# Five input projections of a diffusion block by seven block products instead of eight, with their results kept in DRAM

## The chip, the cores and the metric

One Trainium2 chip, one core of it. The metric is the device time of one execution in microseconds. Three runs of the kernel before took 1818.68, 1819.56 and 1820.62 us (median 1819.56).

## The reference, cut to what matters

One block of a diffusion model on 1024 latent tokens and 256 context tokens, width 1024, all in fp32. `h` is the normed and modulated input, 1024 x 1024.

```python
u, v, q, k, vv, r, af, ab, ga, gb = split(h @ w_in)
b_lat = rmsnorm(gla_scan(q, k, vv, gates(af, ab))) * gla_norm_g * silu(r)     # 4 heads, both directions
v     = layernorm(gelu(v))
a_lat = gelu(u) * (einsum('gpq,bnqgc->bnpgc', w_spatial, v) + b_spatial)
y     = sigmoid(ga) * (a_lat @ w_branch_a) + sigmoid(gb) * (b_lat @ w_branch_b)
x     = x + g1 * (y @ w_out)
a, g  = split(modulate(rmsnorm(x)) @ w_ffn_in)
x     = x + g2 * ((silu(g) * a) @ w_ffn_out)
out   = rmsnorm(x)
```

u, v, r, ga and gb are five products of 1024 x 1024 x 1024 each. g1, g2 and the shifts and scales come from `silu(c) @ w_ada`.

## The kernel before, in words

Every fp32 product is made of three passes of a faster format: each operand is split into a high part (a rounding copy on ACT) and a low part (a subtraction on DVE), and high x high, high x low and low x high are summed in PSUM (`PASS`, L261). A weight tile of 1024 rows by 128 columns is loaded, split by `split_w` (L223 to L231) and multiplied by `mm_fm` (L263 to L266) against the feature-major activations `hT`: 24 matmuls of 512 columns for each half of the tokens. `fm_unit` (L285) is one such tile, 48 matmuls. `tm_unit` (L268) gives token-major results with 256 columns to a matmul; it makes the heads' values and v.

SBUF holds three kinds of buffers that matter here: 40 slots of 4 KB a partition (`slot`, L85) for operands and everything large, 3 raw weight buffers (`raw_w`), and 4 buffers for the split weights. PSUM has 8 banks in two groups of 4.

The order of the work, by program: the first modulation vectors (w_ada) and the context; the norm of x; four heads (L645 to L655, their projections one head ahead); then `gate_b` (L453), which makes r in 8 `fm_unit`s and multiplies the heads' output with silu(r); then a loop (L702) of 8 pairs of units, one for gb and one for branch b, beside which DVE makes the rest of the modulation vectors (`ada_cols`, L670: 32 loads of 512 KB, each with one multiply-add of 1024 columns); then v (L759) by `tm_unit`, beside which `weight_sums` (L742) combines blocks of w_ffn_out and stores them in DRAM, 11 steps of four loads' worth of data; then u with the spatial mixing (L784 to L818, 8 units); then ga and branch a (L841 to L854); then w_out (`project`, L870).

The feed-forward products (L906 to L1198) already use seven block products for eight: both operands are cut in 2 x 2 blocks, sums of blocks are formed and split beforehand, and seven products replace eight. For w_ffn_in, 22 "quads" of 7 x 12 = 84 matmuls each run in one hand-ordered chain on TensorE (`pe`, L863), the first four with part of their products made early while the activations' sums are formed on DVE (L1013 to L1033). w_ffn_out is done in seven `quarter`s (L1103) with operands that are loaded, combined and split on the way.

The compiler's list scheduler orders each engine's instructions by program order and by when it expects operands and buffers to be there; so work from further down may fill gaps, as far as buffers are free. DMAs are issued from SP in one queue; a store that waits for its data holds up what is behind it.

Of the kernel before, what the change touches and what calls it, by code (L numbers as in the profile page):

```python
# [17 lines left out]
P = 128  # L18
T = 1024
# [14 lines left out]
def block_kernel(  # L34
# [39 lines left out]
    small = scope.enter_context(tc.tile_pool(name="small", bufs=2))  # L74
    dram = ctx.enter_context(tc.tile_pool(name="dram", bufs=1, space=bass.MemoryType.DRAM))
# [375 lines left out]
    braw = []  # L451

    def gate_b(h):  # L453

        for fo in (2 * h, 2 * h + 1):
            def evac(ps, hf, fo=fo):
                sl = slice(hf * 512, (hf + 1) * 512)
                sr = small.tile([P, 512], F32, tag="raw", name=nm("sr"), bufs=4)
                nc.scalar.activation(sr, ps, AF.Silu)
                nc.vector.tensor_mul(braw[fo][:, sl], braw[fo][:, sl], sr)  # L460

            fm_unit(w_in, C_R + fo * P, hT.get, evac)
# [30 lines left out]
    def head(h, qq, kk, dec, v, between):  # L493
# [126 lines left out]
        braw.extend(rb)  # L620
# [23 lines left out]
    v = head_products(0, *ahead[:2])  # L644
    for h in range(HEADS):  # L645
        now, ahead = ahead, None

        def between():
            global_next.append(head_gates(h + 1) if h + 1 < HEADS else None)
# [12 lines left out]
    bs = []  # L662
    for h in range(HEADS):
        gate_b(h)
        bs += [split_act(braw[2 * h]), split_act(braw[2 * h + 1])]
# [4 lines left out]
    def ada_cols(chunk, dst):  # L670
# [9 lines left out]
        for hf in range(2):  # L680
            pb = gbank((P, 4, P))
            nc.tensor.matmul(pb, ones, acc[:, hf * 512:(hf + 1) * 512], start=True, stop=True)
            t = small.tile([P, 4, P], F32, tag="raw", name=nm("adat"), bufs=4)
# [14 lines left out]

    mods = [cst.tile([P, 8], F32, name=f"mod{i}") for i in range(4)]
    ada = (step for i in range(4) for step in ada_cols(2 + i, mods[i]))  # L700
    y = []
    for fo in range(KT):  # L702
        sg = slot([P, T])
        fm_unit(w_in, C_GB + fo * P, hT.get, lambda ps, hf: nc.scalar.activation(sg[:, hf * 512:(hf + 1) * 512], ps, AF.Sigmoid))
        [next(ada, None) for _ in range(3 if fo else 0)]

        def evac(ps, hf):
            sl = slice(hf * 512, (hf + 1) * 512)
            nc.vector.tensor_mul(sg[:, sl], ps, sg[:, sl])

        fm_unit(w_branch_b, fo * P, act_get(bs), evac)
        [next(ada, None) for _ in range(2)]
        y.append(sg)
    next(ada, None)
    g1, sh2, s2, g2 = mods
    nc.vector.tensor_scalar(s2, s2, 1.0, None, op0=ALU.add)
    nc.vector.tensor_mul(s2, s2, n2c)


    wsp = slot([P, 8, P])  # L720
    nc.sync.dma_start(wsp, w_spatial.rearrange("g p q -> p g q"))
    wspT = slot([P, 8, P])
    for hf in range(2):
        pt = gbank((P, 4, P))
        for j in range(4):
            nc.tensor.transpose(pt[:, j, :], wsp[:, 4 * hf + j, :], ident)
        nc.scalar.copy(wspT[:, 4 * hf:4 * hf + 4, :], pt)
    bsp = slot([P, 8, P])
    nc.gpsimd.dma_start(bsp.rearrange("p g q -> p (g q)"), b_spatial[0].rearrange("g q -> (g q)").partition_broadcast(P))
    for hf in range(2):  # L730
        pb = gbank((P, 4, P))
        nc.tensor.matmul(pb, ones, wspT[:, 4 * hf:4 * hf + 4, :], start=True, stop=True)
        for j in range(4):
            g = 4 * hf + j
            nc.vector.scalar_tensor_tensor(bsp[:, g, :], pb[:, j, :], lnbc[:, g:g + 1], bsp[:, g, :], op0=ALU.mult, op1=ALU.add)
# [21 lines left out]
    vg = [[slot([P, 4, 256]) for _ in range(2)] for _ in range(4)]  # L757
    stats = small.tile([P, NT, 4, 6], F32, tag="bst", name="bst", bufs=1)
    for gp in range(4):  # L759
        def evac(ps, tp):  # L760
            t = vg[gp][tp // 2][:, 2 * (tp % 2):2 * (tp % 2) + 2, :]
            nc.scalar.activation(t, ps, AF.Gelu)
            for j in range(2):
                nc.vector.bn_stats(stats[:, 2 * tp + j, gp, :], t[:, j, :])

        [next(wsums, None) for _ in range(3)]
        tm_unit(w_in, C_V + gp * 256, hT.get, NT, evac)
# [3 lines left out]
    r = rstd_of(mv[:, :, 1], NT, 1.0)  # L771
    shift = small.tile([P, NT], F32, tag="shift", name="shift", bufs=1)
    nc.vector.scalar_tensor_tensor(shift, mv[:, :, 0], -1.0, r, op0=ALU.mult, op1=ALU.mult)
    for gp in range(4):
        for tt in range(NT):
            t = vg[gp][tt // 4][:, tt % 4, :]
            if tt % 2:
                nc.scalar.activation(t, t, AF.Identity, bias=shift[:, tt:tt + 1], scale=r[:, tt:tt + 1])
            else:
                nc.vector.tensor_scalar(t, t, mv[:, tt, 0:1], r[:, tt:tt + 1], op0=ALU.subtract, op1=ALU.mult)  # L780

    as_ = [None] * KT
    late = {}
    for g in range(8):  # L784
        halves = []

        def evac(ps, hf):
            u = small.tile([P, 512], F32, tag="raw", name=nm("u"), bufs=4)
            nc.scalar.activation(u, ps, AF.Gelu)
            halves.append(u)  # L790

        fm_unit(w_in, C_U + g * P, hT.get, evac)
        if g < 4:
            as_[g] = slot([P, T], F32R), slot([P, T], F32R)
        elif g < 7:
            late[g] = slot([P, T])
        for hf in range(2):
            pm = gbank((P, 4, P))
            for j in range(4):
                nc.tensor.matmul(  # L800
                    pm[:, j, :], vg[g // 2][hf][:, j, (g % 2) * P:(g % 2) * P + P], wspT[:, g, :], start=j == 0, stop=True, skip_group_check=True
                )
            mx = small.tile([P, 4, P], F32, tag="raw", name=nm("mx"), bufs=4)
            nc.vector.scalar_tensor_tensor(mx, pm, lngc[:, g:g + 1], bsp[:, g, :].unsqueeze(1).to_broadcast([P, 4, P]), op0=ALU.mult, op1=ALU.add)
            mx = mx.rearrange("p s i -> p (s i)")
            sl = slice(hf * 512, (hf + 1) * 512)
            a = late[g][:, sl] if g in late else mx
            nc.vector.tensor_mul(a, halves[hf], mx)
            halves[hf] = a
        if g == 7:  # L810
            for i, u in late.items():
                as_[i] = split_act(u)
            as_[g] = slot([P, T], F32R), slot([P, T], F32R)
        if g not in late:
            for hf, a in enumerate(halves):
                hi, lo = (t[:, hf * 512:(hf + 1) * 512] for t in as_[g])
                nc.scalar.copy(hi, a)
# [413 lines left out]
```

## Time and profile before

| | |
|---|---|
| median of 3 runs | 1819.56 us |
| the profiled execution | 1818.25 us, its span 1816.5 us |
| TensorE (PE) busy | 1763.1 us, 97% |
| VectorE (DVE) busy | 982.9 us, 54% |
| ScalarE (ACT) busy | 599.3 us, 33% |
| GpSimd (POOL) busy | 137.5 us, 8% |
| bytes moved by DMA | 201.84 MB, mean 111 GB/s |

The span is the time from the first to the last instruction on the core. The busy shares are of the whole span; stages differ, so rows by stretch of time are needed beside them. A matmul's own duration in the profile is its way through the array (389 ns for 512 columns); matmuls overlap, so the pace is the length of a stretch over the number of matmuls in it.

### The profile page before, as it was taken

Reading aid. Unit: us, or ns where it says so; the run is one execution under the profiler, and the core shown is the slowest. Engines: PE = TensorE matmul, PEld = TensorE weight load, DVE = VectorE, ACT = ScalarE, POOL = GpSimd, SP = SyncE. Lnnn points to the kernel's source line nnn. Section 1 sums busy time; section 2 is a strip of 40 time slices with the busy share of each in tenths; the row PEclk is TensorE's granted clock in tenths of the full one; section 3 lists DMA queues with packets and bytes.
Section 4 is the critical chain, followed back from the end, with each engine's and each line's share of the span. In section 5 each row is a group of like instructions: output and inputs, shape, how many; then the busy total and the mean of one; then the engine's idle time right before and its main releaser. Section 6 shows DMA issues by size and latency. Waiting matters only on the chain. (4 is left out here: it accounts for less than half of the span.)

```text
span 1816.5 us, 22024 instructions
## 1 busy us (share of the span) xinstructions
PE 1763.1 (97%) x8786; PEld 1472.8 (81%) x8786; DVE 982.9 (54%) x1398; ACT 599.3 (33%) x892; POOL 137.5 (8%) x141
## 2 busy tenths in 40 slices
PE   8899999999999999999999999989999999899996
PEld 3887888888888889988888888768888888788885
DVE  7687463643345526553322354895545554556795
ACT  6653432423221112141211222543333332345252
POOL 2220000000000000000000000012121211100001
PEclk9999999999999999999999999999999999999998
DMA  9511001011145439811111242233222222458472
GB/s 341 147 31 35 25 23 36 24 35 35 47 139 183 145 113 320 282 42 40 47 47 47 83 161 81 70 111 99 75 88 81 88 81 81 165 204 288 161 248 93
DMA packets 182871, 201.84 MB, mean 111 GB/s; under 512 B 8624, under 2 KB 132592, under 8 KB 182768
## 3 DMA queue, kind: packets, MB, share of 16 engines
q1 hardware_dynamic: 181952, 199.01, 33.7%
q0 software_dynamic: 720, 1.40, 0.3%
q8 instruction: 69, 1.13, 0.3%
q14 instruction: 34, 0.28, 0.0%
q10 hardware_dynamic: 96, 0.02, 0.0%
HBM read 168.94 MB, written 31.46 MB: 110 GB/s over the span
## 5 line engine op out<-in xcount | busy, mean ns | idle before, releaser
L266 PE MATMUL m<-s,whi 128*128 128x512 f32 (+1 forms) x1856 | 570.9, 388 | 0.7 <-ACT s L488 0.7
L266 PEld LDWEIGHTS m<-s,whi 128*128 128x128 f32 x1856 | 348.0, 189 | 71.5 <-issue 1.4
L266 PE MATMUL m<-s,wlo 128*128 128x512 f32 (+1 forms) x928 | 360.1, 388 | 1.8 <-DVE rstd L164 1.8
L973 PE MATMUL m<-s,s 128*128 128x512 f32 x1320 | 309.5, 391 | 14.2 <-DVE s L910 4.0
L230 DVE TENSOR_TENSOR wlo<-wr,whi 128x1024 fp32r<-128x1024 f32 x106 | 129.8, 1225 | 346.6 <-ACT whi L229 307.1
L973 PEld LDWEIGHTS m<-s,s 128*128 128x128 f32 x1320 | 246.5, 188 | 71.4 <-ACT q L993 5.8
L229 ACT CAST whi<-wr 128x1024 fp32r<-128x1024 f32 x106 | 111.4, 1052 | 441.7 <-PE m L266 306.7
L278 PE MATMUL m<-whi,s 128*128 128x256 f32 x1152 | 218.6, 288 | 0.1
L266 PEld LDWEIGHTS m<-s,wlo 128*128 128x128 f32 x928 | 175.5, 189 | 36.6 <-DVE wlo L230 2.0
L278 PEld LDWEIGHTS m<-whi,s 128*128 128x128 f32 x1152 | 181.8, 192 | 4.5 <-issue 2.9
L278 PE MATMUL m<-wlo,s 128*128 128x256 f32 x576 | 164.6, 286 | 1.3 <-DVE rstd L164 0.8
L278 PEld LDWEIGHTS m<-wlo,s 128*128 128x128 f32 x576 | 110.5, 192 | 3.2 <-DVE wlo L230 1.7
L973 PE MATMUL g<-s,whi 128*128 128x512 f32 x352 | 108.5, 390 | 0.0
L910 DVE TENSOR_TENSOR s<-wr,s 128x1024 fp32r<-128x1024 f32 x77 | 91.1, 1218 | 28.9 <-ACT s L909 28.8
L165 POOL TENSOR_TENSOR rstd<-rstd,nhalf 128x1 f32<-128x1 f32 (+2 forms) x43 | 29.1, 677 | 965.1 <-DVE rstd L164 965.0
L909 ACT CAST s<-wr 128x1024 fp32r<-128x1024 f32 x77 | 78.6, 1054 | 51.3 <-DVE wr L1071 19.0
L910 DVE TENSOR_TENSOR s<-s,s 128x1024 fp32r<-128x1024 f32 x58 | 89.1, 1548 | 6.8 <-ACT s L909 6.8
L909 ACT CAST s<-s 128x1024 fp32r<-128x1024 f32 x58 | 60.5, 1053 | 88.2 <-DVE s L910 41.0
L880 PE MATMUL m<-s,s 128*128 128x512 f32 x384 | 87.5, 389 | 0.0
L880 PEld LDWEIGHTS m<-s,s 128*128 128x128 f32 x384 | 72.0, 188 | 14.9
L1109 PE MATMUL g<-s,s 128*128 128x512 f32 x264 | 81.2, 389 | 0.0
L1109 PE MATMUL m<-s,s 128*128 128x512 f32 x264 | 81.2, 389 | 0.0
(247 smaller groups left out, 2096.4 us busy)
## 6 DMA issues: line engine op xcount, KB each, us to landing
wr<-in_w_in_dram SPq DMA_DIRECT2D x68, 512.0 KB
wr<-in_w_ffn_in_dram SPq DMA_DIRECT2D x48, 512.0 KB
wr<-actd SPq DMA_DIRECT2D x77, 256.0 KB
wr<-in_w_ada_dram SPq DMA_DIRECT2D x32, 512.0 KB
s<-in_w_ffn_out_dram SPq DMA_DIRECT2D x22, 512.0 KB
wsT<-s SPq DMA_DIRECT2D x44, 256.0 KB
wr<-wsT SPq DMA_DIRECT2D x44, 256.0 KB
wr<-in_w_ffn_out_dram SPq DMA_DIRECT2D x33, 256.0 KB
```

The lines of the kernel that those rows point to most:

```text
L165: nc.gpsimd.tensor_tensor(r[:, :n], r[:, :n], nhalf[:, :n], op=ALU.pow)
L229: nc.scalar.copy(hi, raw)
L230: lo_sub[0] = nc.vector.tensor_sub(lo, raw, f(hi)).ins
L266: nc.tensor.matmul(ps, ws[a][:, k, :], get(b, k, t0, n), start=k == 0 and i == 0, stop=k == nk - 1 and i == 2)
L278: nc.tensor.matmul(ps[:, j, :], get(b, 4 * kh + k, (2 * tp + j) * P, P), ws[a][:, k, :], start=kh == 0 and j == 0 and k == 0 and i == 0, s ...
L880: pe(nc.tensor.matmul(ps, yF.get(b, k, tt * P, P), wo[k // 2][a][:, k % 2, :], start=k == 0 and i == 0, stop=k == KT - 1 and i == 2))
L909: nc.scalar.copy(hi, raw)
L910: nc.vector.tensor_sub(lo, raw, f(hi))
L973: pe(nc.tensor.matmul(ps, wts[a][:, k, :], mov[k // 2][b][:, k % 2, :], start=start and k == 0 and i == 0, stop=k == 3 and i == 2, skip_gr ...
L1109: pe(nc.tensor.matmul(banks[tt], o[b][:, 0, tt * P:(tt + 1) * P], o[a][:, 1, :], start=start and k == 0 and i == 0, stop=k == KH - 1 and i ...
```

## The change

r, gb, u and ga no longer go through `fm_unit` but through quads like those of w_ffn_in (7 x 12 matmuls of 512 columns for two column tiles, where there were 2 x 48), 16 quads in one chain; v goes through `wide`, seven products of 48 matmuls of 512 columns, with the tokens as the rows of the result. The moving operands are the blocks of `hT` as they lie split in SBUF (B11, B21, B22); their four sums T1 to T4 are formed on DVE from the high and low parts. All results, and the heads' output, go through DRAM (`rd`, `ud`, `gbd`, `gad`, `vd`, `bd`, `ybd`). The first half of four quads is placed in head 3's program text, between its states and its outputs. After the quads come v (with 7 of the 11 weight-sum steps), then the operands of branch b from `bd` and `rd`, then branch b with the mixing beside it, then branch a with 4 weight-sum steps and all of `ada_cols`. The small pool is closed and opened anew three times instead of once. The feed-forward part uses the same functions as the new quads; its products are the same.

```diff
-    def gate_b(h):
-        for fo in (2 * h, 2 * h + 1):
...
-            fm_unit(w_in, C_R + fo * P, hT.get, evac)
+    bd = proj("bd")
...
-        braw.extend(rb)
+        for fo in range(2):
+            nc.sync.dma_start(bd[2 * h + fo], rb[fo])
...
+    def pe(ins):
+        if last_pe[0] is not None:
+            tc.add_manual_dep(ins.ins, last_pe[0].name, mybir.DependencyInfo(mybir.DependencyClass.NoSync, mybir.DependencyReason.DATA), reason="pe")
...
+    def early_quads(op, todo, between, p1s=(None,) * EARLY):
+        quads = []
+        for fi in range(0, EARLY, 2):
+            pair = [{"ops": weights_a(*weights(todo[fi + i][0], todo[fi + i][1][:1]))} for i in range(2)]
+            for i, q in enumerate(pair):
+                ahead_1(q, op, p1s[fi + i])
+            if fi == 0:
+                between()
+            for q in pair:
+                ahead_2(q, op)
+            quads += pair
+        return quads
+
+    def run_quads(op, todo, quads, hook=None):
+        for fi, (w, cols, sink) in enumerate(todo):
+            if fi < EARLY:
+                if fi:
+                    weights_s(*weights(w, cols), quads[fi]["ops"], nc.vector)
+                others(quads[fi], op, sink)
+            else:
+                va, ga = weights(w, cols)
+                q = {"ops": weights_a(va)}
+                weights_s(va, ga, q["ops"], nc.gpsimd)
+                ahead_1(q, op)
+                others(q, op, sink, lambda: ahead_2(q, op))
...
+    def wide(w, c0, op, sink, hook):
...
+        def product4(banks, name, mov, start, side=()):
+            side = list(side)
+            for kp in range(2):
+                wts = operand(name, kp)
+                for tt in range(4):
+                    for kk in range(2):
+                        for i, (a, b) in enumerate(PASS):
+                            pe(nc.tensor.matmul(banks[tt], op[mov][kp][b][:, kk, tt * P:(tt + 1) * P], wts[a][:, kk, :], start=start and kp == 0 and kk == 0 and i == 0, stop=kp == 1 and kk == 1 and i == 2, skip_group_check=True))
+                if kp == 0:
+                    for s in side:
+                        s()
+            hook()
...
+    def h_first(op):
+        b22, b12 = h_raw(1, 1), h_raw(0, 1)
+        in_place("tensor_sub", b22, b22, b12)
+        op["T3"] = moving(b22)
+        return b22, b12
+
+    def h_others(op, b22, b12, after):
+        b11 = h_raw(0, 0)
+        in_place("tensor_sub", b12, b12, b11)
+        in_place("tensor_add", b11, b11, b22)
+        op["T2"] = moving(b11)
+        after()
+        op["T1"] = moving(b12)
+        b21 = h_raw(1, 0)
+        in_place("tensor_sub", b21, b21, b11)
+        op["T4"] = moving(b21)
...
+    for c0, dst, func in ((C_R, rd, AF.Silu), (C_GB, gbd, AF.Sigmoid), (C_U, ud, AF.Gelu), (C_GA, gad, AF.Sigmoid)):
+        for i in range(0, 8, 2):
+            todo.append((w_in, (c0 + i * P, c0 + (i + 1) * P), to_dram(dst[i:i + 2], func)))
...
+            quads.extend(early_quads(h_op, todo, lambda: None, four()))
+            sums.extend(h_first(h_op))
...
+    h_others(h_op, *sums, lambda: weights_s(*weights(*todo[0][:2]), quads[0]["ops"], nc.vector))
...
+    next_small("small_h")
+    run_quads(h_op, todo, quads)
...
+    wide(w_in, C_V, h_op, v_sink, lambda: next(wsums, None))
...
+    for fo in range(KT):
+        t, s = slot([P, T]), slot([P, T])
+        nc.sync.dma_start(t, bd[fo])
+        nc.sync.dma_start(s, rd[fo])
+        nc.vector.tensor_mul(t, t, s)
+        bs.append(split_act(t))
...
+    for fo in range(KT):
+        def evac(ps, hf):
+            sl = slice(hf * 512, (hf + 1) * 512)
+            t = row512("sgb")
+            nc.sync.dma_start(t, gbd[fo][:, sl])
+            nc.vector.tensor_mul(t, ps, t)
+            nc.sync.dma_start(ybd[fo][:, sl], t)
+
+        fm_unit(w_branch_b, fo * P, act_get(bs), evac)
+        mix(fo)
...
     for fo in range(KT):
...
         def evac(ps, hf):
             sl = slice(hf * 512, (hf + 1) * 512)
...
+            t, yb = row512("sga"), row512("yb")
+            nc.sync.dma_start(t, gad[fo][:, sl])
+            nc.sync.dma_start(yb, ybd[fo][:, sl])
+            nc.vector.tensor_mul(t, ps, t)
+            nc.vector.tensor_add(t, t, yb)
+            hi, lo = (yF.get(part, fo, hf * 512, 512) for part in range(2))
+            nc.scalar.copy(hi, t)
+            nc.vector.tensor_sub(lo, t, f(hi))
+
+        [next(wsums, None) for _ in range(1)]
         fm_unit(w_branch_a, fo * P, act_get(as_), evac)
+        [next(ada, None) for _ in range(5)]
```

In `wide` an operand's tiles are 512 KB loads: one for A11, A12, A22, S2, S1 and S4, two for S3, each for both halves of the depth; S1 to S4 need one combining DVE operation a tile besides the split. `mix(g)` loads two columns' worth of v (`vd`) for every second g and one tile of u (`ud`), scales v, mixes it with 8 matmuls of 128 columns and splits the result. `v_sink` applies the gelu, takes the statistics and stores.

## Rows read from the trace of the kernel before

**Rows 1.** The page: span, busy time by engine, and PE and its clock in 40 slices.
```profile
span 1816.5 us, 22024 instructions
PE 1763.1 (97%) x8786; PEld 1472.8 (81%) x8786; DVE 982.9 (54%) x1398; ACT 599.3 (33%) x892; POOL 137.5 (8%) x141
...
PE   8899999999999999999999999989999999899996
...
PEclk9999999999999999999999999999999999999998
```

**Rows 2.** Busy time by stretch: us, each engine's busy us (instructions), PEclk, DMA share, GB/s.
```profile
404.00:418.00 14.00, 13.30 (x68) 10.88 (x67) 4.38 (x13) 7.88 (x25) 2.77 (x4) 1.00 0.00 1
...
690.00:770.00 80.00, 80.00 (x669) 80.00 (x668) 44.29 (x76) 16.08 (x21) 0.00 (x0) 1.00 0.89 305
787.00:877.00 90.00, 90.00 (x459) 76.73 (x459) 31.70 (x44) 24.95 (x40) 0.00 (x0) 1.00 0.15 41
885.00:1050.00 165.00, 165.00 (x738) 136.90 (x737) 47.46 (x59) 32.50 (x44) 0.00 (x0) 1.00 0.20 58
...
1160.00:1240.00 80.00, 70.51 (x298) 54.81 (x297) 70.72 (x81) 36.10 (x44) 12.33 (x8) 1.00 0.36 109
...
1240.00:1520.00 280.00, 280.00 (x1237) 231.82 (x1237) 150.19 (x175) 89.89 (x117) 58.27 (x45) 1.00 0.27 84
1600.00:1760.00 160.00, 160.00 (x707) 132.50 (x706) 110.75 (x131) 72.38 (x87) 0.62 (x1) 1.00 0.68 235
1660.00:1680.00 20.00, 20.00 (x89) 16.54 (x89) 16.73 (x20) 13.65 (x18) 0.00 (x0) 1.00 0.99 368
1740.00:1760.00 20.00, 20.00 (x90) 16.55 (x89) 19.95 (x26) 11.91 (x13) 0.00 (x0) 1.00 0.87 295
1760.00:1780.00 20.00, 15.82 (x70) 12.76 (x68) 19.09 (x33) 10.13 (x18) 2.33 (x3) 0.98 0.32 114
```

**Rows 3.** PE's groups by line and shape: count | busy us, mean ns | idle before.
```profile
L266 PE MATMUL m<-s,whi 128*128 128x512 f32 x1792 | 555.6, 391 | 0.7 <-ACT s L488 0.7
...
L278 PE MATMUL m<-whi,s 128*128 128x256 f32 x1152 | 218.6, 288 | 0.1
...
L800 PE MATMUL g<-s,s 128*128 128x128 f32 x128 | 15.6, 275 | 0.0
...
L682 PE MATMUL g<-s,ones 128*128 128x512 f32 x16 | 7.5, 591 | 0.0
```

**Rows 4.** DVE's groups by line and shape, columns as in the third group.
```profile
L230 DVE TENSOR_TENSOR wlo<-wr,whi 128x1024 fp32r<-128x1024 f32 x106 | 129.8, 1225 | 346.6 <-ACT whi L229 307.1 <-PE g L800 22.7 <-PE g L682 9.6
...
L910 DVE TENSOR_TENSOR s<-s,s 128x1024 fp32r<-128x1024 f32 x58 | 89.1, 1548 | 6.8 <-ACT s L909 6.8
L678 DVE SCALAR_TENSOR_TENSOR s<-wr,cs,s 128x1024 f32<-128x1024 f32 x32 | 41.1, 1283 | 32.0 <-DMA wr<-in_w_ada_dram 18.9 <-issue 12.8
...
L997 DVE TENSOR_TENSOR u<-m,p 128x512 f32<-128x512 f32 x22 | 15.2, 690 | 24.6 <-PE m L973 24.6
...
L764 DVE BATCH_NORM_STATS2 bst<-s 128x6 f32<-128x256 f32 x32 | 12.3, 418 | 12.8 <-ACT s L762 12.8
...
L684 DVE TENSOR_TENSOR adat<-g,ident 128x512 f32<-128x512 f32 x8 | 5.3, 686 | 5.8 <-PE g L682 5.8
...
L685 DVE TENSOR_REDUCE mod<-adat 128x4 f32<-128x512 f32 x8 | 5.1, 675 | 0.0
```

**Rows 5.** SP's DMA issues in order of time: start, us, line, operation.
```profile
480.78 11.22 SPq L677 DMA_DIRECT2D wr<-in_w_ada_dram  x2
...
677.45 0.34 SPq L745 DMA_DIRECT2D s<-in_w_ffn_out_dram  x1
```

**Rows 6.** DVE's evacuations of branch b, L709: ns min/median/max, first and last start us, shape.
```profile
L709 DVE TENSOR_TENSOR s<-m,s x16: 682/691/692, 516.7 to 681.6; 128x512 f32<-128x512 f32 x16
```

More of the change, by code (lines that the diff above doesn't have):

```diff
@@ L449, in block_kernel, with proj @@
         aft_evac(aft[:, h * 512:(h + 1) * 512], ps)
-    braw = []
-    def gate_b(h):
-        for fo in (2 * h, 2 * h + 1):
[L456 to L460, printed above, removed]
-            fm_unit(w_in, C_R + fo * P, hT.get, evac)
+    def proj(name, n=8):
+        return [dram.tile([P, T], F32, name=f"{name}{i}", tag=f"{name}{i}") for i in range(n)]
+    bd = proj("bd")
     def head_gates(h):
@@ new lines, in product, with tmp, ahead_1 @@
+    def product(ps, wts, mov, start):
+        for k in range(4):
+            for i, (a, b) in enumerate(PASS):
+                pe(nc.tensor.matmul(ps, wts[a][:, k, :], mov[k // 2][b][:, k % 2, :], start=start and k == 0 and i == 0, stop=k == 3 and i == 2, skip_group_check=True))
+    def tmp(s):
+        return small.tile([P, 512], F32, tag="ev", name=nm(s), bufs=ev_bufs)
+    def ahead_1(q, op, p1=None):
+        q["A"] = banks[0]()
+        product(q["A"], q["ops"]["A11"], op["B11"], True)
+        q["p1"] = p1 if p1 is not None else tmp("p1")
+        nc.scalar.copy(q["p1"], q["A"])
@@ new lines, in h_moving, with h_raw, in_place @@
+    def h_moving(j, t):
+        return [(hT.t[0][2 * j + kp][t], hT.t[1][2 * j + kp][t]) for kp in range(2)]
+    def h_raw(j, t):
+        out = []
+        for hi, lo in h_moving(j, t):
+            o = slot([P, 2, 512])
+            nc.vector.tensor_add(o, f(hi), f(lo))
+            out.append(o)
+        return out
+    def in_place(op, dst, xs, ys):
+        for d, a, b in zip(dst, xs, ys):
+            getattr(nc.vector, op)(d, a, b)
+    def h_first(op):
[3 more added lines that the diff above has]
+        return b22, b12
@@ L644, in block_kernel @@
     v = head_products(0, *ahead[:2])
+    quads, sums = [], []
     for h in range(HEADS):
@@ L782, in block_kernel @@
[L782 to L796, printed above, removed]
+    nc.vector.scalar_tensor_tensor(shift, mv[:, :, 0], -1.0, rv, op0=ALU.mult, op1=ALU.mult)
@@ L1086, in block_kernel, with act_sink, sink, f_hook @@
     gen, early = prepared("P1"), []
-    for fi in range(NF):
-        if fi < EARLY:
-            if fi:
-                weights_s(*weights(fi), quads[fi]["ops"], nc.vector)
-            rest(quads[fi], fi)
-        else:
-            va, ga = weights(fi)
-            q = {"ops": weights_a(va)}
-            weights_s(va, ga, q["ops"], nc.gpsimd)
-            first(q)
-            rest(q, fi, lambda: second(q))
-            if fi == NF - 2:
-                g2r = row_of(g2)
-                early = [next(gen)]
+    def act_sink(fi):
+        keep = {}
+        def sink(r, c, src):
+            if r == 2:
+                nc.scalar.activation(src, src, AF.Silu)
+            keep[r, c] = src
+            if (3 - r, c) in keep:
+                dst = keep[2, 1] if c == 1 else keep[1, 2]
+                nc.vector.tensor_mul(dst, keep[1, c], keep[2, c])
+                nc.sync.dma_start(actd[fi][:, half(c)], dst)
+        return sink
+    def f_hook(fi):
+        nonlocal g2r
+        if fi == NF - 2:
+            g2r = row_of(g2)
+            early.append(next(gen))
+    g2r = None
+    todo = [(w_ffn_in, (fi * P, DFF + fi * P), act_sink(fi)) for fi in range(NF)]
+    quads = early_quads(f_op, todo, lambda: block_T(f_blk, xns[4:], 1, bank, f_scale, f_shift))
+    other_operands(f_op, f_blk, lambda: weights_s(*weights(*todo[0][:2]), quads[0]["ops"], nc.vector))
+    run_quads(f_op, todo, quads, f_hook)
     def quarter(gen, banks, start, side=(), per=2):
@@ L1115, in quarter @@
             s()
-    def four():
-        t = [slot([P, 2, 512]) for _ in range(2)]
-        return [t[i // 2][:, i % 2, :] for i in range(4)]
     def residual(tt):
```

443 lines of the change are left out of this document (233 added, 210 removed).

## The prediction

> **What bounds the kernel now.** I read the page first, then busy time by stretch, PE's groups, DVE's groups and SP's issues. The page [rows 1] shows PE busy for 1763.1 of 1816.5 us at a granted clock of nine tenths or more in every slice but the last. So only 53 us are to be had from waits, and whatever shortens the kernel by more must take matmuls away. The stretches [rows 2] show the pace: 1237 matmuls of 512 columns in 280 us are 0.2264 us each, 669 of 256 columns in 80 us are 0.1196 us each. The 389 and 288 ns of [rows 3] are ways through the array and are not added up. No other engine is near its limit in the stages that the change replaces: DVE is busy for 44.3 of 80 us beside v, 31.7 of 90 beside u, 47.5 of 165 beside ga and branch a. DMA is: beside v it is busy 0.89 of the time at 305 GB/s, and this is where the weight sums run.
>
> The same rows show how the scheme behaves where it exists. In steady quads (1240 to 1520) PE is busy for 280 of 280 us, with DVE at 54%. In the quarters (1600 to 1760) it is busy for 160 of 160 with DVE at 69%, and even from 1740 to 1760 with DVE at 19.95 of 20 us. Where sums of activations must be formed first (1160 to 1240), PE loses 9.5 of 80 us with DVE at 70.7; at the last quarter (1760 to 1780) it loses 4.2 of 20 with DVE at 19.1. So the scheme costs PE nothing in its middle and something at each entry, where DVE is full.
>
> **The change, part by part.**
>
> *Matmuls.* r, gb, u and ga are 4 x 384 matmuls now and 4 x 336 after: 192 x 0.2264 = 43.5 us less. v is 768 x 0.1196 = 91.9 us now and 336 x 0.2264 = 76.1 after: 15.8 less. Mixing (15.6 us, L800) and the modulation's matmuls (L682, 7.5) [rows 3] stay. PE's work falls by 59.3 us.
>
> *Entry to the quads.* DVE makes 24 operations of 1024 elements for the four sums (8 rebuild blocks of h, 8 combine, 8 split), at 1.22 (L230) to 1.55 us (L910) [rows 4]: 29 to 37 us. Each early quad adds a weight preparation of some 6.5 us (five operations of 0.69 us, L997, and two of 1.55). PE has 96 early matmuls, 21.7 us, and head 3's own to run meanwhile; DVE idles 9.6 us of 404 to 418 [rows 2], and the first of the sums can be made there. The nearest row is the entry at 1160: 9.5 us lost. Here more of the sums lie beside a head; I take 7, with 0 (all covered) and 20 (28 us that follow the head, less three products of 2.7) as ends. What is queued behind the sums on DVE are the first quads' evacuations, and the chain on PE waits for those.
>
> *Quads.* 84 x 0.2264 = 19.0 us of PE each; DVE has the steady quads' work without two products of 0.69, ACT one more evacuation of 0.6, DMA two more stores of 256 KB. I cost these at nothing: PE covers them, as from 1240 to 1520. If that cover went, DVE's 9 us in 19 still would not be the bound. The 8 stores of the heads' output go to an SP queue whose DMA is idle in that stretch (404 to 418: 0.00), at nothing; behind them are the next head's weights, loaded a head ahead. Two more pool changes are inside the entries' prices.
>
> *v.* DVE beside it: 14 splits and 8 combinations of 1.22, 20 PSUM additions of 0.69, 16 statistics of 512 elements (between 0.42, L764 for 256, and 0.84; I take 0.69, what other operations of 512 take), and 7 weight sums of four operations of 0.69: 27 + 14 + 11 + 19 = 71 us in 76.1. DMA: 8.4 MB of weights (each quarter matrix is read twice), 4.2 of results, 7 x 2.1 of weight sums: 27.3 MB, at the 343 GB/s that 305 at 0.89 makes, 80 us. Both are about full. The rows with DVE this full lose between 0 (1740) and 12% (1160): 0 to 9, and 3 more by DMA. I take 5.
>
> *Entry to branch b.* Its 8 operands can be read and made only when the block sums leave the slots, late in v. They cost 8 x 2 x 1.22 = 19.5 us on DVE behind v's last evacuations, and 8.4 MB, 23 us at 372 GB/s (368 at 0.99 [rows 2]). Each product needs all eight, but four PSUM banks can be advanced as they come, 96 matmuls or 21.7 us. Ends: 2 (all filled) and 26 (nothing filled, and a last split). I take 9: v's last four evacuations and the first operand, during which nothing can be filled.
>
> *Branch b with mixing.* PE 87.0 + 15.6 = 102.6. DVE: 8 x 1.22 for weights, 48 x 0.69, 8 x 1.22 for splits, 16 x 0.42 for scaling: 59. DMA: 4.2 MB in 512-byte rows at 290 GB/s (58 at 0.20, 885 to 1050 [rows 2]) and 16.8 at 372: 60. There is room: 1 us, 0 to 5.
>
> *Branch a with the modulation.* PE 87.0 + 7.5 = 94.5. DVE: weights 9.8, the multiply-adds 41.1 (L678), reductions 10.4 (L684, L685) [rows 4], evacuations 48 x 0.69 = 33, four weight sums 11, splits of w_out 5: 110. DMA: 14.5 for the weights, 16.8 MB of w_ada 45, four weight sums 24.5, ga and branch b's half 22.6, w_out 5.6: 112. So both are some 17 us over PE. Against it stands work that starts ahead: now w_ada's first load, which follows branch b's first unit in the program, is issued at 480.8 and w_ffn_out's, which follows its last, at 677.5 [rows 5], while branch b is evacuated from 516.7 to 681.6 [rows 6]: 36 and 4 us early. I take 8, with 0 and 20 as ends.
>
> *From w_out on*, operations and order are the same: 0. What splits y now lies in branch a's evacuation, where PE waits for nothing at the seam already.
>
> Sum: 7 + 0 + 5 + 9 + 1 + 8 = 30 given back of 59.3. The profiled execution took 1818.25, 1.75 more than its span; 1816.5 - 59.3 + 30 + 1.75 = 1789. The median of the runs is 1.3 above that execution, so I say 1790. With all low ends (2) it is 1761, with all high ends (83) 1842.
>
> **The rivals.**
>
> *Nearly all is kept* (1761 to 1767). For it: PE at 160 of 160 us in the quarters. Against: three entries instead of one, and two stretches in which DVE and DMA have as much to do as PE. Chance 0.12.
>
> *Given back to no change* (1816 to 1823): 54 to 62 us of losses, as by every entry at its high end and v at 12. It needs all look-ahead to fail at once. 0.07.
>
> *Slower: DMA becomes the bound of v and branch a.* There 27.3 + 8.4 and 39.9 MB are to be moved, 75.6 in all, beside 170.6 us of PE. At the 305 GB/s that the stretch beside v shows this takes 248 us; if nothing starts ahead, 77 us are lost, 85 with the other entries, and the time is 1844. It decides where the gain less 8 us is used up: under 341 GB/s without look-ahead, under 293 with the 21.7 and some 15 us of it above. For it: 305 is what was moved at 0.89. Against: 368 GB/s at 0.99 from 1660 to 1680, with loads of 256 KB and PE at 20 of 20, and w_ada in whole rows should go no slower. 0.14.
> The Trainium skill ("DMA: Bandwidth & Descriptors", section "Measured (HBM→SBUF, 128 partitions, SWDGE, issued from GpSimd)") speaks for this rival: it wants transfers of at least 1 MiB and gives 341 GB/s at 1 MB, so that these smaller ones would lie below; at 341 an estimate by that page is 222 us for the 75.6 MB and about 1818 for the kernel. The trace differs, with its 368 GB/s in smaller transfers.
>
> *The early part does not cover the head's end*: the list scheduler puts the sums behind head 3's work and the chain stands still. That is the 20 us end of the entry, 1803, inside the forecast.
>
> **How the numbers follow.** 1768 to 1815, of which 1790 is the middle, has 0.67. Faster by over 0.2% (below 1815.9; about what a measurement can tell here) is 0.67 + 0.12 = 0.79, within it 0.07, slower 0.14. The range for eight in ten leaves out half of the nearly full gain and most of the slower case: 1766 to 1828.
>
> **What the profile after would show.** Right: 4 x 336 matmuls at the quads' pace and 336 of 512 columns for v, PE busy about 1704 us; idle PE of 5 to 10 us each after head 3, at the seam from v to branch b and in the first four units of branch a, ended by DVE splits or weight loads; a DMA share over 0.85 beside v and branch a. Wrong: PE idle in steady quads, which would mean that stores hold up the weights on SP or that slots run out; a pace of v's matmuls other than 0.226; or more than 50 us of new idle time in v and branch a ended by DMA.

## The result, and the profile after

The changed kernel takes 1872.19 us (median of 4 runs, 1870.62 to 1872.89) against 1819.80 us before: a ratio of 1.0287, with an interval of 1.0269 to 1.0305. It is slower by 52 us where 30 us less was forecast, and outside the range. The profiled execution after took 1870.62 us.

The page after, with the rows that answer to [rows 1], and the DMA rows of the slices:

```profile
span 1868.9 us, 21551 instructions
PE 1729.4 (93%) x8162; PEld 1415.0 (76%) x8162; DVE 1141.5 (61%) x1563; ACT 669.7 (36%) x974; POOL 192.3 (10%) x181
...
PE   8899999997999999969957779989999999999996
...
PEclk9999999998999999989978889999999999999998
DMA  9501102112533335897678761133222223368572
```

A slice is 46.7 us. Three places show in the PE row: the tenth slice, at 7, after the heads; the eighteenth, at 6, from 794 us; and four of 5, 7, 7, 7 from 934 us on. Only in the last does the granted clock stay down for several slices, and there the DMA row stands at 7, 8, 7, 6: not full. The span grew by 52.4 us. PE's idle time grew from 1816.5 - 1763.1 = 53.4 to 1868.9 - 1729.4 = 139.5 us, by 86.1; PE's busy time fell by only 33.7 of the 59.3 us that were worked out. 86.1 - 33.7 = 52.4, so these two carry all of it.

Busy time by stretch after, columns as in [rows 2]:

```profile
420.00:500.00 80.00, 65.41 (x281) 50.91 (x280) 63.60 (x82) 39.83 (x66) 13.07 (x10) 0.94 0.41 122
500.00:740.00 240.00, 240.00 (x1060) 198.74 (x1059) 108.16 (x121) 89.18 (x123) 43.46 (x35) 1.00 0.41 123
740.00:780.00 40.00, 40.00 (x178) 32.99 (x177) 25.61 (x32) 15.39 (x20) 0.00 (x0) 1.00 0.75 268
780.00:860.00 80.00, 64.53 (x252) 48.00 (x251) 59.80 (x81) 26.23 (x31) 3.24 (x2) 0.91 0.86 299
860.00:940.00 80.00, 79.85 (x412) 67.43 (x411) 49.65 (x79) 21.40 (x28) 0.00 (x0) 1.00 0.72 236
...
940.00:960.00 20.00, 11.61 (x55) 9.38 (x53) 12.38 (x17) 2.29 (x3) 0.99 (x2) 0.87 0.91 328
960.00:980.00 20.00, 5.89 (x15) 4.25 (x16) 15.90 (x17) 1.05 (x1) 0.00 (x0) 0.53 0.80 249
...
820.00:840.00 20.00, 11.98 (x32) 7.75 (x33) 8.76 (x9) 5.05 (x5) 1.65 (x2) 0.76 1.08 373
940.00:1100.00 160.00, 103.53 (x395) 78.90 (x394) 107.50 (x128) 20.87 (x26) 1.96 (x4) 0.81 0.75 248
```

Set beside the sum of the prediction, PE's idle time by stretch is:

| step | stretch | priced (ends) | idle after |
|---|---|---|---|
| entry to the quads | 420 to 500 | 7 (0 to 20) | 14.6 |
| quads, first half of v | 500 to 780 | 0 | 0 |
| rest of v, entry to branch b | 780 to 860 | 5 + 9 (2 to 38) | 15.5 |
| branch b with mixing | 860 to 940 | 1 (0 to 5) | 0.2 |
| branch a with the modulation | 940 to 1100 | 8 (0 to 20) | **56.5** |

Together 86.8 us, which is as much as the idle time grew (86.1). Branch a alone is outside its ends. It also holds most of the matmuls' lost gain: of its 395 matmuls 16 are the modulation's (7.5 us) and 23 small ones (2.8 us by their own durations, which is an upper bound); the other 356 take 80.6 us at 0.2264. That makes 90.9 us where 103.5 were spent, 12.6 more, at a mean clock of 0.81. By the same reckoning 780 to 860 lost 7 us, at a mean clock of 0.91.

What PE waits for there, from the waits after (who waited for whom: total us, times, longest), the first row for the whole span, the next two for PE and SP's queue from 930 to 1100 us:

```profile
PE m L273 <- ACT whi L236: 62.5, 6, 22.5
...
PE m L273 <- ACT whi L236: 56.3, 5, 22.5
...
SPq L976 <- DVE s L977: 34.8, 23, 8.0
```

All of branch a's idle time (56.3 of 56.5 us) is one kind of wait: its matmuls (L273) for the high part of a weight tile (L236). That split is late since its load is late, and the trace in order of time says why. SP's issues, and in the second fence DVE's and PE's work (start us, us, line, operation, idle before and its releaser):

```profile
902.70 0.33 SPq L976 DMA_DIRECT2D wr<-in_w_ada_dram  x1
...
915.76 0.33 SPq L976 DMA_DIRECT2D wr<-in_w_ada_dram  x1
...
928.45 0.33 SPq L976 DMA_DIRECT2D wr<-in_w_ada_dram  x1
...
962.13 2.12 SPq L976 DMA_DIRECT2D wr<-in_w_ada_dram  x2
...
966.68 0.49 SPq L261 DMA_DIRECT2D wr<-in_w_branch_a_dram  x1
...
1059.33 0.38 SPq L261 DMA_DIRECT2D wr<-in_w_branch_a_dram  x1
```

```profile
953.80 0.69 DVE L1129 TENSOR_TENSOR s<-sga,s 128x512 fp32r<-128x512 f32 x1 [0.74 <-ACT s L1128]
954.66 0.91 DVE L972 MEMSET s<- 128x1024 f32 x1 [0.16 <-issue]
...
960.81 1.28 DVE L977 SCALAR_TENSOR_TENSOR s<-wr,cs,s 128x1024 f32<-128x1024 f32 x1 [4.17 <-DMA s<-in_b_ada_dram]
...
974.07 1.22 PE L273 MATMUL m<-s,whi 128*128 128x512 f32 x2 [22.46 <-ACT whi L236]
```

Three loads of w_ada are issued beside branch b, at 902.7, 915.8 and 928.5. They take all three raw weight buffers. Their consumer, the multiply-add (L977), needs the sum that the memset at 954.7 starts and that b_ada's DMA completes; its first run is at 960.8. The trace gives the memset itself no wait: on DVE it stands right behind the last evacuation of branch a's first unit (L1129), and slots were being filled anew from 942.0 on, by a weight sum's load. So the order on DVE held it at the end; whether want of a slot held it earlier is not shown. Until 960.8 no raw buffer comes free, and branch a's second weight tile is issued at 966.7, after two more w_ada loads. PE stands for 22.5 us. From then on branch a's tiles are issued at 966.7 and, five units later, at 1059.3: 18.5 us a unit where its matmuls need 48 x 0.2264 = 10.9. Between two of them go some five loads of w_ada through the same three buffers: six loads in 18.5 us, 3.1 us each. The schedule asks for six in 10.9 us, 1.8 each. In the kernel before, a pair of units took 21.7 us with two weight tiles and up to five steps of `ada_cols`, which is also 3.1 us a load, and PE lost nothing there, as this row of the kernel before shows:

```profile
505.00:545.00 40.00, 40.00 (x178) 33.14 (x177) 17.96 (x18) 6.89 (x9) 0.56 (x1) 1.00 0.49 151
```

Neither engine nor memory is full meanwhile: DVE is busy for 107.5 of 160 us, DMA for 0.75 at 248 GB/s. The Trainium skill ("Perfetto Trace Analysis", section "Optimization Strategy") says that consistent bubbles on the engine that should be saturated can mean that there is not enough memory for the next tile, and names the buffer count. This trace agrees, with a wait for the weights five times in 160 us and three buffers.

### The profile page after: what moved, and what is told of

It reads as the page before. It is cut to its first block, busy times and chain, and to the rows that moved or that the text cites. A ratio compares the mean times of both kernels' runs of the same rounds, so it can differ in the third digit from the quotient of the medians.

```text
span 1868.9 us, 21551 instructions
## 1 busy us (share of the span) xinstructions
PE 1729.4 (93%) x8162; PEld 1415.0 (76%) x8162; DVE 1141.5 (61%) x1563; ACT 669.7 (36%) x974; POOL 192.3 (10%) x181
## 5 line engine op out<-in xcount | busy, mean ns | idle before, releaser
L273 PE MATMUL m<-s,whi 128*128 128x512 f32 (+1 forms) x832 | 268.0, 403 | 70.5 <-ACT whi L236 62.5
L716 PE MATMUL m<-s,s 128*128 128x512 f32 x1320 | 309.6, 391 | 14.0 <-DVE s L638 4.0
L273 PEld LDWEIGHTS m<-s,whi 128*128 128x128 f32 x832 | 162.1, 199 | 108.5 <-ACT whi L236 65.6
L716 PE MATMUL g<-s,s 128*128 128x512 f32 x960 | 226.0, 392 | 12.4 <-ACT s L637 6.8
L716 PEld LDWEIGHTS g<-s,s 128*128 128x128 f32 x960 | 180.4, 189 | 53.9 <-ACT s L637 7.1
L236 ACT CAST whi<-wr 128x1024 fp32r<-128x1024 f32 x92 | 96.6, 1053 | 228.4 <-PE m L273 81.2
L273 PE MATMUL m<-s,wlo 128*128 128x512 f32 (+1 forms) x416 | 165.9, 399 | 2.2 <-DVE rstd L171 1.8
L285 PE MATMUL m<-whi,s 128*128 128x256 f32 x640 | 125.3, 290 | 0.1
L285 PEld LDWEIGHTS m<-whi,s 128*128 128x128 f32 x640 | 101.3, 191 | 4.3 <-issue 2.7
L273 PEld LDWEIGHTS m<-s,wlo 128*128 128x128 f32 x416 | 82.1, 197 | 21.8 <-DVE wlo L237 6.3
L285 PE MATMUL m<-wlo,s 128*128 128x256 f32 x320 | 92.0, 287 | 1.6 <-DVE wlo L237 1.6
L1158 PE MATMUL m<-s,s 128*128 128x512 f32 x384 | 87.5, 389 | 0.0
```

The lines of the kernel that those rows point to most:

```text
L273: nc.tensor.matmul(ps, ws[a][:, k, :], get(b, k, t0, n), start=k == 0 and i == 0, stop=k == nk - 1 and i == 2)
L285: nc.tensor.matmul(ps[:, j, :], get(b, 4 * kh + k, (2 * tp + j) * P, P), ws[a][:, k, :], start=kh == 0 and j == 0 and k == 0 and i == 0, s ...
L716: pe(nc.tensor.matmul(ps, wts[a][:, k, :], mov[k // 2][b][:, k % 2, :], start=start and k == 0 and i == 0, stop=k == 3 and i == 2, skip_gr ...
L1158: pe(nc.tensor.matmul(ps, yF.get(b, k, tt * P, P), wo[k // 2][a][:, k % 2, :], start=k == 0 and i == 0, stop=k == KT - 1 and i == 2))
```

## The experiments

Three theories of branch a were set against each other: **ring** (the three raw buffers, shared by urgent weights and w_ada in SP's order), **bytes** (DMA is the bound) and **DVE** (its amount of work). The first four kernels ran once each, beside the kernel before at 1817.98 us. Kernels that ran several times spread by 2 to 9 us from run to run, so that a difference of a few us between single runs is not clear by itself. No run gave the ring a fourth buffer.

**ada_slots**: w_ada goes to slots of its own, not to the raw buffers.

```diff
-            w = raw_w([P, D])
+            w = slot([P, D])
             nc.sync.dma_start(w, w_ada[k * P:(k + 1) * P, chunk * D:(chunk + 1) * D])
```

> The changed kernel with one line different: w_ada's loads go into slots instead of the three raw weight buffers; bytes, operations and program order are the same. Theory ring (w_ada's loads hold the raw buffers, so branch a's weights are loaded late and PE waits): the 56 us of idle PE between 940 and 1100 fall under 25 and the slow clock there goes, so 1820 to 1840 us. Theory bytes (the 40 MB of that stretch bound it): unchanged, 1860 to 1875. Theory DVE (its 110 us bound it): unchanged, 1860 to 1875.

Measured 1849.16 us, 23 less than the changed kernel and 9 above what ring gave. PE's waits:

```profile
PE m L273 <- ACT whi L236: 17.9, 3, 10.7
PE g L981 <- DVE s L977: 17.5, 1, 17.5
```

The wait for weights fell from 62.5 to 17.9 us, as ring says. PE's idle time from 940 to 1100 us fell less, from 56.5 to 35.8 us, where ring gave under 25. The rest went to a wait that no theory had: the modulation's matmul (L981) now stands in PE's queue ahead of its sum, and everything behind it stood for 17.5 us.

**ada_order**: branch a's weights are fetched one unit ahead in the program, so that they come before the five w_ada loads; bytes and operations are the same.

```diff
+    ws_next = load_fm(w_branch_a, 0)
     for fo in range(KT):
...
-        fm_unit(w_branch_a, fo * P, act_get(as_), evac)
+        ws_a, ws_next = ws_next, load_fm(w_branch_a, (fo + 1) * P) if fo + 1 < KT else None
+        for hf in range(2):
+            ps = bank()
+            mm_fm(ps, ws_a, act_get(as_), hf * 512, 512)
+            evac(ps, hf)
```

> The changed kernel, but branch a's weights are loaded and split one unit ahead of their matmuls in the program, so ahead of five w_ada loads; bytes and buffers are the same. Theory ring: the first wait for weights (22.5 us) goes and the later ones shrink, 1835 to 1855 us. Theory bytes: 1862 to 1875, since the same bytes pass in the same stretch. Theory DVE: 1862 to 1875.

Measured 1841.48 us, inside what ring gave. The stretch of branch a:

```profile
940.00:1100.00 160.00, 132.75 (x548) 103.71 (x547) 122.27 (x150) 28.41 (x34) 1.96 (x4) 0.91 0.84 286
```

and PE's wait for weights:

```profile
PE m L273 <- ACT whi L236: 32.2, 6, 14.7
```

In the same 160 us DMA moved more (286 GB/s, was 248) and DVE did more (122 us, was 107), and PE did 548 matmuls for 395. So neither was the bound at 248 GB/s and 107 us. This is the run that parts ring from the other two. The first long wait, which ring had go, shrank to 14.7 us: three w_ada loads (918.3, 930.9 and 943.6) still go out ahead of branch a's third tile (972.6). From there to the tile five units later (1054.0) the ring passes 30 loads in 81.4 us, 2.7 us each.

**sums_quads**: the four weight sums of branch a (24.5 us of DMA and 11 of DVE by the prediction) move beside the quads.

```diff
-    run_quads(h_op, todo, quads)
...
     wsums = weight_sums()
+
+    run_quads(h_op, todo, quads, lambda fi: fi in (5, 8, 11, 14) and next(wsums))
```

> The changed kernel with all eleven weight-sum steps moved: four beside the quads (after quads 5, 8, 11 and 14), the other seven beside v as before, none beside branch a. It takes 8.4 MB and 11 us of DVE out of branch a. Theory bytes: 25 us less, 1842 to 1852. Theory DVE: 11 us less, 1858 to 1864. Theory ring: w_ada's loads still hold the buffers, 1860 to 1872.

Measured 1868.33 us, as ring gave: 16 us over the range of bytes, but only 4 over that of DVE, which one run does not part. The first 60 us of branch a:

```profile
940.00:1000.00 60.00, 42.93 (x181) 34.12 (x180) 37.46 (x42) 5.52 (x7) 0.98 (x2) 0.83 0.59 185
```

and PE's wait for weights over the span:

```profile
PE m L273 <- ACT whi L236: 53.2, 6, 17.0
```

With DMA at 0.59 and 185 GB/s PE is still idle for 17 of 60 us, and the wait for weights is still 53 us. Fewer bytes do not help while the order stays.

**ada_quads**: all of w_ada moves beside the quads, three loads behind each, whose stretch was full on PE with DVE at 45%.

```diff
-    run_quads(h_op, todo, quads)
...
+    def h_hook(fi):
+        if fi >= EARLY:
+            [next(ada, None) for _ in range(3)]
+
+    run_quads(h_op, todo, quads, h_hook)
...
         fm_unit(w_branch_a, fo * P, act_get(as_), evac)
-        [next(ada, None) for _ in range(5)]
```

> The changed kernel with the rest of the modulation (32 loads of w_ada with their multiply-adds) moved from branch a to the quads, three steps after each from the fifth on. All three theories of branch a let its idle PE go, 1790 to 1815 us, if the quads, with PE at 100%, DVE at half and DMA at 0.38, cover the steps. If the quads don't cover them (raw buffers shared with the quads' weights), PE is idle there and the time stays over 1830.

Measured 1852.48 us, so the quads did not cover it. The stretch of the quads:

```profile
500.00:740.00 240.00, 217.19 (x900) 172.03 (x899) 147.80 (x158) 79.44 (x110) 56.85 (x36) 0.97 0.54 164
```

and two of PE's waits, for what ACT and DVE make of the products:

```profile
PE m L716 <- ACT p L725: 11.2, 6, 4.6
PE g L716 <- DVE u L740: 8.1, 3, 4.5
```

Branch a is clean (60 of 60 us from 1000 to 1060), but the quads lose 22.8 of 240 us with DVE at 62%. These two, with 3.6 us of a third of the kind (L743), are all of it; none is a wait for weights, so the raw buffers that the quads share with w_ada are not what PE waits for directly. DVE has time left, but from 500 to 740 us it stands still for 42.1 us, in 12 waits of its multiply-add (L977) for w_ada's loads, and evacuations come behind those in DVE's order: at 573.8 the multiply-add starts after 4.9 us, the evacuation (L740) follows at 576.1, and PE goes on at 576.8. My "costed at nothing" for the quads holds for the load that they had, not for any.

The next four ran beside 1819.27 us.

**acc_early**: the first sum's slot is taken and filled ahead of branch b, so that the three early loads can be used up at once. The loads and their order in the program stay.

```diff
+    acc0 = acc_of(2)
     for fo in range(KT):
...
+        acc = acc0 if chunk == 2 else acc_of(chunk)
```

> The changed kernel, but the first sum of the modulation gets its slot and its bias before branch b instead of beside branch a. In the trace of the changed kernel w_ada's first three loads are issued beside branch b and fill the three raw buffers, while the multiply-add that would release them waits for a slot until 955. Theory held ring (that wait is what delays branch a's second weights by 22.5 us): the first wait goes, 1842 to 1856 us. Theory rate (w_ada's loads through three buffers are simply slower than five in a unit's 11 us): the wait only moves on, 1864 to 1872.

Measured 1852.96 us, inside what the held ring gave. PE's wait for weights:

```profile
PE m L273 <- ACT whi L236: 33.9, 7, 9.7
```

The longest wait fell from 22.5 to 9.7 us and the total from 62.5 to 33.9. The ring now runs on beside branch b: by 942 us nine w_ada loads are issued, where there were three, and branch a's second tile goes out at 925.1 instead of 966.7. So the 19 us (1872.2 to 1853.0) are the price of the held ring together with six loads that no longer fall beside branch a; the two are not parted. What is left of the wait comes with the tiles issued from 966.9 on.

**spread**: 14 of the 32 w_ada loads go beside the quads, one each, the rest beside branch a three to a unit, with its weights fetched ahead as in ada_order. That is four loads in 10.9 us, 2.7 each.

```diff
+    def h_hook(fi):
+        if fi >= 2:
+            [next(ada, None) for _ in range(1)]
...
+        ws_a, ws_next = ws_next, load_fm(w_branch_a, (fo + 1) * P) if fo + 1 < KT else None
...
-        [next(ada, None) for _ in range(5)]
+        [next(ada, None) for _ in range(3)]
```

> The changed kernel with branch a's weights one unit ahead (as in the second run) and w_ada's steps spread: one after each quad from the third on (14) and three instead of five a unit beside branch a. Theory rate (raw buffers pass about one load in 2.5 us): quads pass 3 loads in 19 us and units 4 in 11, so both are covered, idle PE between 500 and 740 under 3 us and in branch a under 12, 1800 to 1816 us. Theory that any w_ada step beside branch a costs PE (one queue, any order): branch a keeps 25 us of idle time, 1825 to 1840.

Measured 1820.27 us, 52 less than the changed kernel and 4 above the expectation; the quads lost 4.7 of 240 us, where under 3 was expected. The seam from v to branch b, and branch a:

```profile
780.00:860.00 80.00, 65.19 (x257) 49.99 (x256) 59.49 (x83) 23.49 (x28) 3.27 (x2) 0.91 0.95 333
...
940.00:1060.00 120.00, 114.21 (x491) 91.01 (x490) 93.39 (x122) 25.18 (x31) 0.98 (x2) 0.97 0.85 287
```

Branch a loses 5.8 of 120 us at 287 GB/s, more than the 248 at which it lost 56.5 of 160. The seam from v to branch b is left as it was.

**spread_ws**: as spread, with all weight sums of v beside the quads too.

```diff
+        if fi >= 5:
+            next(wsums, None)
```

> As the run before, and all eleven weight-sum steps beside the quads, one after each from the sixth on, none beside v or branch a. Beside v this takes 14.7 MB and 19 us of DVE away. If DVE and DMA beside v make the idle time from v into branch b (15.5 us from 780 to 860 in the changed kernel), it falls under 8 and the time is 10 to 20 us under the run before, 1785 to 1803. If that entry is set by the order of loads and splits of branch b's operands alone, it stays at 13 to 16 us, and the time is that of the run before less at most 5.

Measured 1817.13 us, 3 less than spread, which single runs hardly tell apart. Neither case came out: the seam's idle time fell under 8 us, as in the first, and the time stayed as in the second. The quads and the seam:

```profile
500.00:740.00 240.00, 228.49 (x967) 181.20 (x968) 157.90 (x172) 83.88 (x119) 52.66 (x35) 0.99 0.69 222
...
780.00:860.00 80.00, 73.14 (x315) 58.05 (x313) 54.69 (x73) 29.54 (x37) 2.26 (x2) 1.00 0.72 237
```

The seam's idle time is 6.9 us (15.5 in the changed kernel, 14.8 in spread), and branch a has none from 940 to 1100 us. So DVE's work and the bytes beside v make about half of the seam's wait. But the quads lose 11.5, and branch b 2.6 of 80 us. DVE is busy for 66% of the quads' stretch; that the place of its operations costs PE there, as in ada_quads, is likely and was not tested.

**s_first**: at the entry after head 3, the first quads' weight sums are made ahead of the activations' sums.

```diff
     def h_others(op, b22, b12, after):
+        after()
         b11 = h_raw(0, 0)
...
-        after()
```

> The changed kernel with the first quad's weight preparation on DVE ahead of the sums T2, T1 and T4 in the program instead of between T2 and T1. After head 3, PE waits 6.9 us for that preparation's split. Theory DVE order: the first product starts some 5 us earlier and later products wait for T2 and T1 instead, 2 to 5 us less in all, 1866 to 1870. Theory DVE amount (all sums must pass anyway): within 1.5 us of the changed kernel, 1870 to 1874.

Measured 1877.20 us, 5 us slower than the changed kernel, which neither case had. The entry after:

```profile
420.00:500.00 80.00, 66.79 (x266) 51.78 (x266) 62.81 (x81) 38.48 (x65) 12.84 (x9) 0.91 0.38 113
```

PE is busy for 1.4 us more than in the changed kernel, but it does 266 matmuls there for 281, at a lower granted clock (0.91, was 0.94). By 780 us it has done 3831 for 3846, which is 3.4 us at 0.2264 each. So most of the 5 us lie at the entry and not in branch a, which only comes later. Two runs that leave the entry as it was stand at 3836 (ada_slots) and 3841 (ada_order), so that one run does not settle how much of it is the order.

The next two ran 7 and 8 times, beside 1818.45 us.

**late**: spread, and the early halves of the first quads placed behind head 3 in the program.

```diff
-            quads.extend(early_quads(h_op, todo, lambda: None, four()))
             sums.extend(h_first(h_op))
...
+    quads.extend(early_quads(h_op, todo, lambda: None, four()))
```

> The run with w_ada's steps spread (1820 us), and the early halves of the first four quads in the program after head 3 instead of between its states and outputs; only T3 stays there. Theory order (in the changed kernel the 21.7 us of early matmuls are used up by 417, before DVE has time for the sums, and PE stands at head 3's end): the head ends some 18 us earlier, the early matmuls lie beside the sums, idle PE from head 3 to the steady quads falls from 16.5 to 8 us or less, 1806 to 1814 us. Theory amount (DVE's 35 us of sums and preparations after the head set the entry, wherever the early matmuls lie): within 3 us of 1820.

Measured 1823.24 us, ratio to before 1.0026 (1.0014 to 1.0037): nearer to what the amount of work gave (and just outside it) than to what the order gave. From 400 to 500 us PE is idle for 16.0 us, and for 16.5 in spread.

**mixed**: late, with four of v's seven weight sums beside the quads and three left beside v; branch a's four begin two units later.

```diff
+        if fi in (6, 9, 12, 15):
+            next(wsums)
...
+    in_v = [1, 1, 1]
+    wide(w_in, C_V, h_op, v_sink, lambda: in_v and in_v.pop() and next(wsums))
```

> The run before, with the eleven weight-sum steps divided: 4 beside the quads (after quads 7, 10, 13 and 16), 3 beside v, 4 beside branch a's last units. If the idle time from v into branch b comes from DVE and DMA being full beside v, as the run with all sums in the quads suggests (15 us there became 7), and a step in every third quad is covered: 5 to 9 us under the run before, 1798 to 1808 us. If the steps cost as much wherever they lie: the same as the run before.

Measured 1813.65 us, ratio 0.9980 (0.9969 to 0.9991). It is 6 us above the range, which was counted from the time expected of late; against late as measured it is 9.6 us less, which is what a covered step gave (5 to 9). It is 0.2% faster than the kernel before. In the same stretches:

```profile
500.00:740.00 240.00, 235.04 (x1022) 192.58 (x1023) 135.80 (x154) 88.62 (x124) 52.07 (x35) 0.99 0.57 177
...
780.00:860.00 80.00, 73.10 (x303) 55.93 (x302) 57.66 (x78) 27.89 (x34) 2.26 (x2) 0.98 0.72 243
...
940.00:1100.00 160.00, 152.28 (x665) 122.60 (x664) 107.61 (x140) 29.43 (x36) 1.53 (x3) 0.99 0.73 245
```

The last row is worth setting beside that of the changed kernel: the same 107.5 us of DVE and the same 245 to 248 GB/s in 160 us, and PE does 665 matmuls for 395. The sums of bytes and of DVE's time do not set this wait.

The last two ran beside 1819.01 us, no_ada once and mixed_early 10 times.

**no_ada**: the changed kernel without w_ada beside branch a.

```diff
-    ada = (step for i in range(4) for step in ada_cols(2 + i, mods[i]))
+    for m in mods:
+        nc.vector.memset(m, 1.0)
+    ada = iter(())
```

> The changed kernel without the rest of the modulation: its 32 loads, multiply-adds, matmuls and reductions are left out and g1, g2 and the second shift and scale are constants. It prices what w_ada's steps cost beside branch a. If they are the cause of nearly all the idle time there (56 us between 940 and 1100) and of the slow clock with it: 65 to 80 us less than the changed kernel, 1792 to 1807 us, and PE waits under 8 us for branch a's weights. If branch a's own reads from DRAM or the four weight-sum steps have a part: 1810 to 1840 us.

Measured 1809.48 us, between the two cases. The price of w_ada in that place is 1872.2 - 1809.5 = 63 us, of which the modulation's own matmuls are 7.5. Two stretches of branch a:

```profile
940.00:1000.00 60.00, 60.00 (x274) 49.81 (x273) 41.37 (x58) 13.59 (x17) 0.00 (x0) 1.00 0.89 300
1000.00:1060.00 60.00, 50.01 (x220) 40.91 (x219) 26.55 (x34) 13.80 (x17) 0.00 (x0) 0.91 0.52 178
```

PE's wait for weights over the span, of which only the longest is in branch a:

```profile
PE m L273 <- ACT whi L236: 17.7, 2, 10.0
```

and SP's issues before it, then ACT's splits and PE, in order of time:

```profile
991.24 0.95 SPq L1112 DMA_DIRECT2D wr<-in_w_out_dram  x2
...
999.55 0.38 SPq L1112 DMA_DIRECT2D wr<-in_w_out_dram  x1
...
1024.17 0.38 SPq L261 DMA_DIRECT2D wr<-in_w_branch_a_dram  x1
...
1020.71 2.93 ACT L236 CAST s<-wr 128x1024 fp32r<-128x1024 f32 x3
...
1030.44 1.22 PE L273 MATMUL m<-s,whi 128*128 128x512 f32 x2 [9.96 <-ACT whi L236]
```

First, DMA moves 300 GB/s at 0.89 with PE at 60 of 60 us, which theory bytes does not allow. Second, the remaining 10 us are the same mechanism once more: three loads of w_out at 991 to 1000 take the raw buffers and are split only at 1020.7, and branch a's last weight tile is issued behind them at 1024.2. This reading is the trace's alone; no run moved w_out's loads. With w_ada out of the ring (ada_slots) the wait for weights came to 17.9 us, here to 17.7.

**mixed_early**: mixed, with the early halves inside head 3 again.

```diff
             quads.extend(early_quads(h_op, todo, lambda: None, four()))
             sums.extend(h_first(h_op))
...
-    quads.extend(early_quads(h_op, todo, lambda: None, four()))
```

> The run with the weight sums divided (1813.7 us), with the early halves of the quads back between head 3's states and outputs, as in the change. If their place does not matter, as the run with them moved suggests against the one before it: within 3 us, 1810 to 1816 us. If moving them cost the 3 us that lay between those two: 1808 to 1811.

Measured 1816.79 us, 0.8 above the expectation, ratio 0.9991 (0.9981 to 1.0000). Its interval overlaps that of mixed, so where the early halves stand is not told apart.

## Why the prediction was wrong

*Matmuls.* The number was right: 8786 instructions became 8162, the quads run 1060 in 240 us (0.2264), and v 178 in 40 (0.2247). Busy time came to 1729.4 us instead of 1704: of the missing 25.6 us 12.6 lie in branch a and 7 in 780 to 860, where matmuls run at a lower granted clock after waits; where the other 6 lie was not worked out. The sum priced each wait by its length alone.

*Entry to the quads.* 14.6 us, inside 0 to 20 but twice the 7 taken. Neither the place of the early halves nor the order of the sums made it cheaper; behind head 3 DVE is full:

```profile
436.00:455.00 19.00, 11.20 (x39) 8.11 (x40) 18.93 (x21) 10.43 (x12) 1.49 (x1) 0.73 0.38 124
```

So the rival in which the sums stand behind head 3's work, with its 20 us, came about in part. How to hide the entry stays open.

*Quads.* At nothing, as priced, for the load they carry here. ada_quads and spread_ws show how near the edge they are.

*v and the entry to branch b.* 15.5 us for 14. In mixed, with fewer weight sums beside v, 6.9 us remain.

*Branch b with mixing.* 0.2 us for 1.

***Branch a with the modulation*** is the step that failed. It priced DVE (110 us) and DMA (112) against PE (94.5) and took 8 us, with 20 as the upper end. Measured were 56.5 us of idle time, all of it for weights, and 12.6 us of slow matmuls. The amounts were about right and decide nothing: the step left out the three raw buffers and SP's order. Its sentence that look-ahead helps, since now w_ada's first load is issued 36 us early [rows 5, 6], was the wrong way round: with their sum not begun before 954.7, three loads issued 36 to 58 us before their use shut the ring for branch a's weights. The count that shows it was at hand: 7 loads in 21.7 us before, 6 in 10.9 after, through the same three buffers. acc_early (19 us), ada_order (31 us with the same bytes) and no_ada (63 us) price the parts; they overlap and are not added.

*The rivals.* The slower one had the sign and not the cause. It asked for DMA at its limit in v and branch a; branch a ran at 0.75 and 248 GB/s, still lost 47.5 of the same 160 us at 197 (sums_quads), and lost little at 287 (spread). The Trainium skill's rule for it ("DMA: Bandwidth & Descriptors", section "Measured (HBM→SBUF, 128 partitions, SWDGE, issued from GpSimd)") wants at least 1 MiB a transfer; no run here tried that size, and the trace has 373 GB/s from 820 to 840 us with smaller ones. Of the two other rivals, nearly all kept and no change, neither came about.

*What the profile after was to show.* PE idle in v and branch a was named as a sign of error if over 50 us and ended by DMA. It was over 50 us, but ended by a split behind a late issue: a wait for a buffer, which has no row in the shares of DMA and DVE.

## What to carry to other kernels

Where a background stream shares a ring of buffers with the weights that PE waits for, count loads per buffer and per unit of PE time before counting bytes: here the change asked for one load in 1.8 us and got one in 3.1. That is no fixed rate of three buffers: with the urgent tile ahead in the order (ada_order) they passed one in 2.7. A load issued ahead helps only if its consumer can run; if that has to wait, here for a sum not yet begun, the load holds a buffer that others need. So its consumer's own needs must be met first, or the urgent load must stand ahead of it in the queue. The weight sums spread thinly over three stages (mixed) cost 9.6 us less than beside v and branch a alone (late).

## What the runs showed of the hardware that was not expected

Waits cost more than their length. After the 22.5 us wait of branch a, whose first row stands above (974.07), three more of PE's rows in order of time:

```profile
978.48 0.77 PE L273 MATMUL m<-s,whi 128*128 128x512 f32 x2
...
979.32 0.62 PE L273 MATMUL m<-s,whi 128*128 128x512 f32 x2
...
981.39 0.62 PE L273 MATMUL m<-s,whi 128*128 128x512 f32 x2
```

and the stretch ahead of them, columns as in [rows 2]:

```profile
960.00:974.00 14.00, 0.00 (x0) 0.00 (x0) 11.15 (x13) 1.03 (x1) 0.00 (x0) 0.50 0.76 238
```

While PE stood idle the granted clock was 0.50, the lower of its two levels (1.2 of 2.4 GHz). From 974.07 to the row at 978.48 nine matmuls start, 0.49 us each; from 979.32 to 981.39 another nine, 0.23 each. Over the kernel PE's busy time is 25.6 us above the 1704 that the prediction worked out, nearly half of the loss against the kernel before; 19.6 of it lie in branch a and in 780 to 860.
